# Last stage of a decoder step: LayerNorm rows broadcast by DMA instead of spread by TensorE, and part of VectorE's row work moved to GpSimd

## The chip, the cores and the metric

One NeuronCore of a Trainium2 chip runs the whole kernel. The metric is device time in microseconds of one execution; a profiled execution also leaves a trace of every instruction. Engines: PE (TensorE), DVE (VectorE), ACT (ScalarE), POOL (GpSimd), SP (SyncE, which here only issues DMAs and waits).

## The reference, cut to what matters

The kernel is one layer of a hybrid decoder for 512 prompt tokens and 32 sample tokens, all in float32. The stage that changes computes what follows the first LayerNorm:

```python
x = layer_norm(DN_ALPHA * x + mix, ln_g[0], ln_b[0])
x = layer_norm(DN_ALPHA * x + hier_moe(x, ...), ln_g[1], ln_b[1])      # 32 experts, top 2 of one group
ple = jax.nn.sigmoid(x @ w_pg) * (p_i @ w_pp)
x = layer_norm(DN_ALPHA * x + ple, ln_g[2], ln_b[2])
```

`x` is 544 x 1024, `w_pg` 1024 x 1024. The products with `w_pg` are made from high and low halves of both sides (three matmuls for one), so each side is first split into a rounded copy and the rest.

## The kernel before, in words

The prompt's tokens are handled as NT = 4 tiles of 128 rows x 1024 columns (`x1s[0]` to `x1s[3]`), the 32 sample tokens as one tile of 128 x 256 (`x1q`, with the helpers that end in `_q`).

**The expert phase** (`expert_phase`) is one critical section: each engine runs its own hand-written program, ordered by semaphores, and the planner sees the section as one block. Weights lie in four slots; SyncE refills them, and once a slot's last expert is done (`late`), it loads what the next stage needs into the freed room: the four `x1s` tiles, LN1's gain `gain1`, and one half of `w_pg`. TensorE does gate and up products (L302), a transpose (L307) and the down product (`psY`, L316) of each expert; GpSimd scatters each result to `ybuf` in DRAM. Behind the last expert TensorE spreads LN2's gain and shift over 128 partitions (`spread_half`, L148: a matmul with a broadcast column of the identity, from the 48 x 128 tile `gb`), four halves into PSUM, and ScalarE copies each out (L449). VectorE multiplies the four `x1s` tiles by `gain1` (L526). Each engine raises `fin` when it is done; SyncE waits for the last scatters (L237), for its late loads, and for `fin` of all four (L240). Only then does any engine go on.

**The last stage** follows in the planner's own order (`issue_after` places some instructions behind others of the same engine). SyncE loads the experts' results for each tile (`rows_of_experts`, two tiles of 128 x 1024 for each t), the other half of `w_pg`, and the embeddings' products. The order of the work:

- TensorE runs products that nothing reads (`keep_busy`, L2115: eight matmuls of 256 columns, which the trace lists as 16 records), spreads LN3's gain and shift (`spread`, L2107 for ScalarE's copies), and runs eight more.
- ScalarE casts the first half of `w_pg` in eight chunks of 128 x 512 (L577) and VectorE takes the rest (L578): the split of chunk k.
- `moe_norm(0)`: VectorE adds the two experts' results (L2130, L2131; the second leaves the row sum `total`), ScalarE makes the sum of squares (L2122), GpSimd the power -1/2 (L2124), VectorE the two last operations (L1771, L1772).
- `turn(0)`: TensorE transposes the tile (L2145), ScalarE and VectorE split it (L2146, L2147).
- The second half of `w_pg` is split (L2245, L2247), then `moe_norm(1)`.
- For each tile `embed_norm`: 2 x 8 x 3 matmuls (`three`, L690 to L692), a sigmoid, the product with the embedding, LN3 and the store; between them the norm and the turn of the next tiles and the sample rows.

Of the kernel before, what the change touches and what calls it, by code (L numbers as in the profile page):

```python
# [9 lines left out]
F32 = mybir.dt.float32  # L10
# [9 lines left out]
P = 128  # L20
# [122 lines left out]

def spread_half(pe, ident, rows, out, first):

    n = rows.shape[0]
    for k in range(4):
        m = pe.matmul(out[:, P * k:P * (k + 1)], ident[0:n, first + k:first + k + 1].to_broadcast([n, P]), rows[:], start=True, stop=True)  # L148
    return m


def expert_phase(tc, pool, psum, ident, meta, slots, x1, W, w, ybuf, spare, gcol, late, rows, spreads, xs, any_):

# [25 lines left out]
    names = [f"{n}{i}" for n in ("gu", "gv", "wd", "we") for i in range(NB)]  # L179
    names += "gh gi gx tx c4 cx gu xa xb rb se sc ra sl hh th ch dn cy iy y0 y1 y2 y3 al fin gz".split()  # L180
    with tc.tile_critical(no_gpsimd_drain=True):
# [188 lines left out]
        pe.matmul(psY[:], ident, any_, start=True, stop=True)  # L370
        npp, full, gap = value(pe, 80, NB, 32), value(pe, 81, 0, 32 // NB - 1), value(pe, 84, 0, NB - 1)
        with pe.If(full > 0):
            with pe.Fori(0, full) as a:
                for s in range(NB):
                    items_of(a, s, pe.snap(a * NB + s), turn_before(a) if s == 0 else
                             lambda i: down_of(s - 1, i, pe.snap(a + 1)))
        full1 = pe.snap(full + 1)
        for s in range(NB):
# [15 lines left out]
            else:  # L394
                items_of(full, s, p, prev)
        it = value(pe, 82, 1, 66)
        pe.wait_ge(S["hh"], pe.snap(it + 1))
        transpose_h()
        down_of(NB - 1, it, full1)

        halves = [(out[:, 512 * i:512 * (i + 1)], which + 4 * i) for out, which in spreads for i in range(2)]
        banks = [psX[:, 4 * i:4 * i + 4].rearrange("p k t -> p (k t)") for i in range(2)]
        for n, (_, which) in enumerate(halves):
            if n > 1:
                pe.wait_ge(S["sc"], n - 1)
            spread_half(pe, ident, rows, banks[n % 2], which).then_inc(S["se"], 1)
        pe.sem_inc(S["fin"], 1)
# [38 lines left out]
        act.activation(out=tiny, in_=gcol[:, 0, 0:1], func=AF.Sigmoid)  # L446
        for n, (out, _) in enumerate(halves):
            act.wait_ge(S["se"], n + 1)
            act.copy(out=out, in_=banks[n % 2]).then_inc(S["sc"], 1)  # L449
        act.wait_ge(S["sc"], len(halves))  # L450
        act.sem_inc(S["fin"], 1)
# [81 lines left out]
def tile_decoder_step(ctx: ExitStack, tc: tile.TileContext, *aps):  # L533
# [1113 lines left out]
    gcol8 = const.tile([P, 2, KD], F32, name="gcol8")  # L1647
    gb = const.tile([6 * KD, P], F32, name="gb")
    const.tile([P, 8], F32, name="edgel")
# [61 lines left out]
    act.mul(out=shift1, in_=shift1, mul=0.5)  # L1711
    for j, n in enumerate(("ln_g", "ln_b")):
        gp.dma_start(out=gb[24 * j:24 * j + 24], in_=A[n][0].rearrange("i (k d) -> (i k) d", k=KD))

# [118 lines left out]
    with ExitStack() as scope:  # L1833
# [203 lines left out]
        with tc.issue_after(table.ins):  # L2037
# [17 lines left out]
    gbq = [t.rearrange("p (j d) -> p j d", j=2) for t in gbq]  # L2055
    gain2, shift2, gain3, shift3 = (r_p[:, i] for i in range(4))

    pg_half = lambda i: (pg_in[i], A["w_pg"][0, :, 512 * i:512 * (i + 1)].rearrange("(k p) f -> p k f", p=P))
    late = [(0, [(x1s[t], x1d[t * P:(t + 1) * P], "rb") for t in range(NT)] + [(gain1, A["ln_g"][0, 0].partition_broadcast(P), "rb"),
                                                                                         (*pg_half(0), "al")])]  # L2060
    spreads = [(gain2, 8), (shift2, 32)]
    with ExitStack() as scope:

        SP_ = pool("spare", stack=scope)
        spare = SP_.tile([P, D], F32, name="xg"), SP_.tile([P, 2, KD, P], F32, name="xg4")
        gp.indirect_dma_start(out=spare[0], out_offset=None, in_=x1d[:], in_offset=bass.IndirectOffsetOnAxis(ap=tok0[:, 0:1], axis=0))
        expert_phase(tc, pool("xwork", side="right", stack=scope), pool("expp", space=PSUM, stack=scope), ident, meta,
                     (tok, yrow, ywt, shift1, gain1), x1d[:], w_tiles, w_e, ybuf[:], spare, gcol8, late, gb, spreads, x1s,
                     keep[:, 0:256])
# [30 lines left out]

    def spread(out, i):

        for half in range(2):
            cs = slice(512 * half, 512 * (half + 1))
            po = ps2.tile([P, 512], F32, name="po")
            m = spread_half(pe, ident, gb, po, i + 4 * half)
            act.copy(out=out[:, cs], in_=po)  # L2107
        return m

    def keep_busy(n, behind=None):  # L2110

        idle = ps2.tile([P, 256], F32, name="pp", bufs=1)
        with tc.issue_after(behind.ins) if behind else nullcontext():
            for _ in range(n):
                m = pe.matmul(idle, ident, keep[:, 0:256], start=True, stop=True)  # L2115
        return m

# [8 lines left out]
    def moe_norm(t):  # L2126
        x2 = x1s[t]
        y1, y2 = held[t]
        total = TL.tile([P, 1], F32, name="total", bufs=4)
        dve.tensor_tensor(out=x2, in0=x2, in1=y1, op=ALU.add)  # L2130
        dve.scalar_tensor_tensor(out=x2, in0=y2, scalar=1.0, in1=x2, op0=ALU.mult, op1=ALU.add, accum_out=total)  # L2131
        stats = full_stats(x2, total, y2, EPS2)
        if t:
# [61 lines left out]
    def moe_norm_q():  # L2195
        dve.tensor_tensor(out=x1q, in0=x1q, in1=gbq[0][:, 0], op=ALU.mult)
        for i in range(2):
            dve.tensor_tensor(out=x1q, in0=x1q, in1=yq[:, i], op=ALU.add)
        norm_q(x1q, 0)
# [19 lines left out]
    sy.dma_start(out=pg_half(1)[0], in_=pg_half(1)[1])  # L2219
    rows_of_experts(1)  # L2220
    for out, src in ((embeds[:, 0:512], pld[P:2 * P, 512:]), (embeds[:, 512:512 + D], pld[2 * P:3 * P])):
        sy.dma_start(out=out, in_=src)
    rows_of_experts(2)
    rows_of_experts(3)
    for out, src in ((embeds[:, 512 + D:], pld[3 * P:4 * P]), (pls, plsd[:]), (x1q, x1d[SEQ:].rearrange("t (q d) -> q t d", q=4)),
                     *((yq[:, i], ybuf[NG * i + SEQ:NG * (i + 1)].rearrange("t (q d) -> q t d", q=4)) for i in range(2))):
        dma = sy.dma_start(out=out, in_=src)
    busy = keep_busy(8)
    for k in range(KD):
        cast = split_from(pg(k, 0, 0, 512), pg(k, 1, 0, 512), pg_in[0][:, k])  # L2230
    with tc.issue_after(busy.ins), tc.issue_after(cast.ins):
        spread(gain3, 16)
        busy = spread(shift3, 40)
    keep_busy(8, busy)
    with tc.issue_after(dma.ins):
# [6 lines left out]
    for k in range(KD):  # L2242
        H, L, src = pg(k, 0, 512, D), pg(k, 1, 512, D), pg_in[1][:, k]
        with tc.issue_after(high.ins):
            act.copy(out=H, in_=src)  # L2245
        with tc.issue_after(low.ins):
            lows = dve.tensor_tensor(out=L, in0=src, in1=H.bitcast(F32), op=ALU.subtract)  # L2247
    for t in range(1, NT + 2):
        if t <= NT:
            if t < NT:  # L2250
                with tc.issue_after(applied.ins if t > 1 else lows.ins):
                    behind, applied = moe_norm(t)
            if t == NT - 2:
                with tc.issue_after(applied.ins):
                    moe_norm_q()
# [39 lines left out]
```

## Time and profile before

| | us |
|---|---|
| median of 3 runs | 1138.86 (1135.3 to 1141.66) |
| the profiled execution: time | 1140.12 |
| its span, from first to last instruction | 1138.2 |
| PE busy | 1046.4 (92%) |
| DVE busy | 487.4 (43%) |
| ACT busy | 346.7 (30%) |
| POOL busy | 249.9 (22%) |

Times of the profile count from the start of the span. The shares are means over stages that differ: the expert phase waits for weights, the last stage (from about 1040 us) for one engine after another. A row of the timeline gives start, duration, engine, line, operation and operands, and in brackets the idle time before it with what ended it. The granted clock is the share of its full clock that TensorE was given.

### The profile page before, as it was taken

How to read it: one execution, taken by the hardware profiler on the slowest of the kernel's cores; microseconds unless marked ns; L12 is line 12 of the kernel's file. 1: busy time of each engine (PE TensorE's matmuls, PEld its weight loads, DVE VectorE, ACT ScalarE, POOL GpSimd, SP SyncE). 2: the span in 40 equal slices, each digit the busy share in tenths (PEclk: the TensorE clock that was granted, in tenths of full speed). 3: DMA queues.
4: the chain of work that ended last, by engine and by line, in shares of the span. 5: the costliest groups of instructions: out<-in, count | busy, mean ns of one | idle time of the engine just before them, and what ended most of it. 6: DMA issues, size and time to landing. Idle time of an engine off the chain costs nothing.

```text
span 1138.2 us, 26943 instructions
## 1 busy us (share of the span) xinstructions
PE 1046.4 (92%) x10391; PEld 817.4 (72%) x10392; DVE 487.4 (43%) x1255; ACT 346.7 (30%) x702; POOL 249.9 (22%) x379
## 2 busy tenths in 40 slices
PE   9999999999999999999999877696998979977987
PEld 8988999999877779999989444343555545544765
DVE  5545543456545556554665511110111111112787
ACT  5411123232666665323213111110222111111531
POOL 5000001301346562223301102210222212211021
PEclk9999999999999999999999889987999999988888
DMA  7222222224214334654396989999999999997711
GB/s 249 76 75 75 75 74 75 79 75 132 80 37 149 111 114 142 208 158 102 122 413 256 372 310 414 422 416 425 415 422 418 420 420 419 422 419 304 282 46 61
DMA packets 99296, 264.18 MB, mean 232 GB/s; under 512 B 11470, under 2 KB 58852, under 8 KB 85364
## 3 DMA queue, kind: packets, MB, share of 16 engines
q1 hardware_dynamic: 84868, 234.05, 53.9%
q0 software_dynamic: 9696, 25.31, 6.2%
q10 hardware_dynamic: 4656, 3.77, 1.1%
q8 instruction: 53, 0.87, 0.3%
q14 instruction: 23, 0.19, 0.1%
HBM read 248.96 MB, written 20.13 MB: 236 GB/s over the span
## 4 chain that ended last, share of the span: by engine, by line
PE 75%; DMA 10%; SPq 7%; issue 3%; DVE 3%; ACT 1%; DVEq 0%; POOL 0%; ACTq 0%; POOLq 0%
PE pj L690 14%; PE pj L692 13%; PE pj L691 13%; PE psG L302 10%; SPq L135 5%; PE psY L316 5%; DMA gu3b<-in_w_eu_dram 5%; PE tp L1285 2%; DMA w<-in_w_eu_dram 2%; DMA w2b<-in_w_eu_dram 2%; SPq L141 2%; PE sp L1331 1%; PE nm L1319 1%; PE sp L748 1%; PE po L692 1%
## 5 line engine op out<-in xcount | busy, mean ns | idle before, releaser
L690 PE MATMUL pj<-xH,wH 128*128 128x256 f32 (+1 forms) x672 | 197.6, 294 | 0.1
L692 PE MATMUL pj<-xH,wL 128*128 128x256 f32 (+1 forms) x672 | 197.4, 294 | 0.0
L691 PE MATMUL pj<-xL,wH 128*128 128x256 f32 (+1 forms) x672 | 195.6, 291 | 0.0
L577 ACT CAST wH<-raw 128x1024 fp32r<-128x1024 f32 x76 | 79.7, 1049 | 232.3 <-PE pj L691 148.1
L690 PEld LDWEIGHTS pj<-xH,wH 128*128 128x128 f32 x672 | 126.5, 188 | 5.5 <-issue 3.8
L692 PEld LDWEIGHTS pj<-xH,wL 128*128 128x128 f32 x672 | 126.4, 188 | 5.5 <-issue 5.1
L691 PEld LDWEIGHTS pj<-xL,wH 128*128 128x128 f32 x672 | 127.0, 189 | 2.0 <-issue 1.5
L578 DVE TENSOR_TENSOR wL<-raw,wH 128x1024 fp32r<-128x1024 f32 x76 | 95.2, 1252 | 69.4 <-ACT wH L577 69.2
L302 PE MATMUL psG<-w,xT 128*32 128x256 f32 x1152 | 77.1, 410 | 25.1 <-issue 16.8
L434 ACT ACTIVATE sg<-psG 128x128 f32<-128x128 f32 x50 | 13.9, 277 | 270.3 <-PE psG L302 270.3
L465 DVE COPY hT<-psH 128x128 f32<-128x128 f32 x50 | 14.6, 292 | 153.3 <-PE psH L307 151.4
L302 PEld LDWEIGHTS psG<-w,xT 128*32 128x32 f32 x1152 | 38.4, 116 | 55.2 <-issue 36.1
L1307 POOL TENSOR_SCALAR lg<-lg,sm 128x256 f32<-128x256 f32 (+1 forms) x64 | 55.8, 886 | 32.6 <-DVE sm L1304 28.6
L460 DVE COPY xT<-xg 128x256 f32 x49 | 14.5, 295 | 111.8 <-PE psG L302 111.8
L265 POOL DMA_INDIRECT ybuf<-ysb,idy x50 | 49.6, 992 | 45.8 <-POOL idy L262 40.1
L302 PE MATMUL psG<-gu3a,xT 128*32 128x256 f32 x576 | 36.7, 395 | 15.5 <-DMA gu3a<-in_w_eu_dram 9.5
L472 DVE SCALAR_TENSOR_TENSOR ysb<-psY,ywt,r_p 128x256 f32<-128x256 f32 x50 | 24.2, 483 | 56.8 <-PE psY L316 56.8
L690 PE MATMUL pj<-wH,xH 128*128 128x256 f32 x160 | 47.3, 296 | 0.0
L416 ACT ACTIVATE xg<-psX,gcol 128x128 f32 (+1 forms) x100 | 36.4, 469 | 33.6 <-PE psX L295 33.6
L692 PE MATMUL pj<-wH,xL 128*128 128x256 f32 x160 | 44.8, 280 | 0.0
L691 PE MATMUL pj<-wL,xH 128*128 128x256 f32 x160 | 44.7, 280 | 0.0
L302 PE MATMUL psG<-gu3b,xT 128*32 128x256 f32 x576 | 38.2, 410 | 6.1 <-DMA gu3b<-in_w_eu_dram 6.1
(615 smaller groups left out, 2265.3 us busy)
## 6 DMA issues: line engine op xcount, KB each, us to landing
w<-in_w_eg_dram SPq DMA_DIRECT2D x26, 1024.0 KB, 20.6
w<-in_w_eu_dram SPq DMA_DIRECT2D x26, 1024.0 KB, 23.1
w<-in_w_ed_dram SPq DMA_DIRECT2D x26, 1024.0 KB, 24.6
raw<-in_w_in_dram SPq DMA_DIRECT2D x22, 1024.0 KB
w2d<-in_w_ed_dram SPq DMA_DIRECT2D x14, 1024.0 KB, 24.4
r_p<-in_w_ed_dram SPq DMA_DIRECT2D x14, 1024.0 KB, 22.4
w2a<-in_w_eg_dram SPq DMA_DIRECT2D x7, 1024.0 KB, 22.4
w2a<-in_w_eu_dram SPq DMA_DIRECT2D x7, 1024.0 KB, 26.6
```

The costliest lines, as they stand in the source:

```text
L135: return [eng.dma_start(out=W[s][half][:, i], in_=w[i][bass.ds(e, 1)].rearrange("a (p k) f -> (a p) k f", p=P)[:, ks]) for i in range(2)]
L265: gp.indirect_dma_start(out=ybuf.rearrange("t (q d) -> (t q) d", q=4), out_offset=bass.IndirectOffsetOnAxis(ap=idy[:, r:r + 1], axis=0), i ...
L302: m = pe.matmul(psG[32 * q:32 * q + 32], xT[:, k], W[s][half][:, :, kh, P * q:P * q + P], start=k == 0, stop=k == KD - 1)
L316: m = pe.matmul(psY[32 * q:32 * q + 32], hT[:, 32 * k:32 * k + 32], W[s][2][:, k, 256 * q:256 * q + 256], start=k == 0, stop=k == 3)
L416: m = act.activation(out=out, in_=psX[:, k], func=AF.Identity, bias=gcol[:, 1, k:k + 1], scale=gcol[:, 0, k:k + 1])
L472: dve.scalar_tensor_tensor(out=ysb[:, r], in0=psY[:], scalar=ywt[:, bass.ds(i1, 1)], in1=shift, op0=ALU.mult, op1=ALU.add).then_inc(S["cy" ...
L577: act.copy(out=H, in_=src)
L578: return eng.tensor_tensor(out=L, in0=src, in1=H.bitcast(F32), op=ALU.subtract)
L690: pe.matmul(out, lh(k), rh(k), start=start and i == 0, stop=False)
L691: pe.matmul(out, lh(k), rl(k), start=False, stop=False)
L692: pe.matmul(out, ll(k), rh(k), start=False, stop=stop and i == len(ks) - 1)
L1307: gp.tensor_scalar(out=lg[:, par, j, 0:nk], in0=lg[:, par, j, 0:nk], scalar1=sm[:, 2, par, j:j + 1], scalar2=None, op0=ALU.mult)
```

## The change

In the expert phase the spreads go, with their copies and semaphores. LN2's gain and shift come by DMA, each as one row read 128 times, queued by SyncE behind the last experts of slots 1 and 2; SyncE waits for them (`al`) at the end. TensorE issues ten products that nothing reads, and loads one register earlier. VectorE multiplies only `x1s[0]` by `gain1` there.

In the last stage LN3's gain and shift come by DMA, behind the second tile's results. The first batch of products grows from 8 to 14; the second batch is made from `total` of the first tile and so waits for it. GpSimd takes over: `gain1` on the other three tiles, the splits of chunks 5 to 7 of the first half and 4 to 7 of the second, the first add of tiles 2 and 3, and three operations on the sample rows. `moe_norm(1)` is placed behind VectorE's fourth split of the second half instead of the eighth.

```diff
@@ expert_phase
+        it = value(pe, 82, 1, 66)
         with pe.If(full > 0):
...
-        it = value(pe, 82, 1, 66)
         pe.wait_ge(S["hh"], pe.snap(it + 1))
         transpose_h()
         down_of(NB - 1, it, full1)
-        for n, (_, which) in enumerate(halves):
-            if n > 1:
-                pe.wait_ge(S["sc"], n - 1)
-            spread_half(pe, ident, rows, banks[n % 2], which).then_inc(S["se"], 1)
+        for _ in range(10):
+            pe.matmul(psX[:, 0:2].rearrange("p k t -> p (k t)"), ident, any_, start=True, stop=True)
         pe.sem_inc(S["fin"], 1)
...
-        for n, (out, _) in enumerate(halves):
-            act.wait_ge(S["se"], n + 1)
-            act.copy(out=out, in_=banks[n % 2]).then_inc(S["sc"], 1)
-        act.wait_ge(S["sc"], len(halves))
         act.sem_inc(S["fin"], 1)
@@ tile_decoder_step
-    gb = const.tile([6 * KD, P], F32, name="gb")
...
-    for j, n in enumerate(("ln_g", "ln_b")):
-        gp.dma_start(out=gb[24 * j:24 * j + 24], in_=A[n][0].rearrange("i (k d) -> (i k) d", k=KD))
...
-    gain2, shift2, gain3, shift3 = (r_p[:, i] for i in range(4))
+    gain2, shift2, gain3, shift3 = row(W1, 11), row(w2a, 2), r_p[:, 2], r_p[:, 3]
...
-                                                                                         (*pg_half(0), "al")])]
-    spreads = [(gain2, 8), (shift2, 32)]
+                                                                                         (*pg_half(0), "al")]),
+            (1, [(gain2, A["ln_g"][0, 1].partition_broadcast(P), "al")]), (2, [(shift2, A["ln_b"][0, 1].partition_broadcast(P), "al")])]
...
-                     (tok, yrow, ywt, shift1, gain1), x1d[:], w_tiles, w_e, ybuf[:], spare, gcol8, late, gb, spreads, x1s,
+                     (tok, yrow, ywt, shift1, gain1), x1d[:], w_tiles, w_e, ybuf[:], spare, gcol8, late, x1s[0:1],
...
-    def keep_busy(n, behind=None):
+    def keep_busy(n, by=ident):
         idle = ps2.tile([P, 256], F32, name="pp", bufs=1)
-        with tc.issue_after(behind.ins) if behind else nullcontext():
-            for _ in range(n):
-                m = pe.matmul(idle, ident, keep[:, 0:256], start=True, stop=True)
-        return m
+        for _ in range(n):
+            pe.matmul(idle, by, keep[:, 0:256], start=True, stop=True)
@@ moe_norm
-        dve.tensor_tensor(out=x2, in0=x2, in1=y1, op=ALU.add)
+        if t < 2:
+            dve.tensor_tensor(out=x2, in0=x2, in1=y1, op=ALU.add)
         dve.scalar_tensor_tensor(out=x2, in0=y2, scalar=1.0, in1=x2, op0=ALU.mult, op1=ALU.add, accum_out=total)
+        if t == 0:
+            keep_busy(8, total[:, 0:1].to_broadcast([P, P]))
@@ moe_norm_q
-        dve.tensor_tensor(out=x1q, in0=x1q, in1=gbq[0][:, 0], op=ALU.mult)
+        gp.tensor_tensor(out=x1q, in0=x1q, in1=gbq[0][:, 0], op=ALU.mult)
         for i in range(2):
-            dve.tensor_tensor(out=x1q, in0=x1q, in1=yq[:, i], op=ALU.add)
+            gp.tensor_tensor(out=x1q, in0=x1q, in1=yq[:, i], op=ALU.add)
@@ the last stage
     rows_of_experts(1)
+    for out, m in ((gain3, A["ln_g"]), (shift3, A["ln_b"])):
+        sy.dma_start(out=out, in_=m[0, 2].partition_broadcast(P))
...
-    busy = keep_busy(8)
+    keep_busy(14)
+    gp.tensor_tensor(out=x1s[1], in0=x1s[1], in1=gain1, op=ALU.mult)
     for k in range(KD):
-        cast = split_from(pg(k, 0, 0, 512), pg(k, 1, 0, 512), pg_in[0][:, k])
-    with tc.issue_after(busy.ins), tc.issue_after(cast.ins):
-        spread(gain3, 16)
-        busy = spread(shift3, 40)
-    keep_busy(8, busy)
+        low = split_from(pg(k, 0, 0, 512), pg(k, 1, 0, 512), pg_in[0][:, k], gp if k > 4 else dve)
+        if k == 4:
+            cast = low
...
         with tc.issue_after(low.ins):
-            lows = dve.tensor_tensor(out=L, in0=src, in1=H.bitcast(F32), op=ALU.subtract)
+            lows = (dve if k < 4 else gp).tensor_tensor(out=L, in0=src, in1=H.bitcast(F32), op=ALU.subtract)
+        if k == KD // 2 - 1:
+            halfway = lows
     for t in range(1, NT + 2):
         if t <= NT:
             if t < NT:
-                with tc.issue_after(applied.ins if t > 1 else lows.ins):
+                with tc.issue_after(applied.ins if t > 1 else halfway.ins):
                     behind, applied = moe_norm(t)
+            if t == 1:
+                for later in (2, 3):
+                    with tc.issue_after(behind.ins):
+                        gp.tensor_tensor(out=x1s[later], in0=x1s[later], in1=gain1, op=ALU.mult)
+                        gp.tensor_tensor(out=x1s[later], in0=x1s[later], in1=yall[2 * later], op=ALU.add)
```

More of the change, by code (lines that the diff above doesn't have):

```diff
@@ L141, in load_dn, with expert_phase @@
     return eng.dma_start(out=W[s][2][:, ks], in_=w[2][bass.ds(e, 1)].rearrange("a (k p) d -> p (a k) d", p=P)[:, ks])
[L144 to L148, printed above, removed]
-    return m
-def expert_phase(tc, pool, psum, ident, meta, slots, x1, W, w, ybuf, spare, gcol, late, rows, spreads, xs, any_):
+def expert_phase(tc, pool, psum, ident, meta, slots, x1, W, w, ybuf, spare, gcol, late, xs, any_):
     nc = tc.nc
@@ L179, in expert_phase @@
     names = [f"{n}{i}" for n in ("gu", "gv", "wd", "we") for i in range(NB)]
-    names += "gh gi gx tx c4 cx gu xa xb rb se sc ra sl hh th ch dn cy iy y0 y1 y2 y3 al fin gz".split()
+    names += "gh gi gx tx c4 cx gu xa xb rb ra sl hh th ch dn cy iy y0 y1 y2 y3 al fin gz".split()
     with tc.tile_critical(no_gpsimd_drain=True):
@@ L399, in expert_phase @@
         down_of(NB - 1, it, full1)
-        halves = [(out[:, 512 * i:512 * (i + 1)], which + 4 * i) for out, which in spreads for i in range(2)]
-        banks = [psX[:, 4 * i:4 * i + 4].rearrange("p k t -> p (k t)") for i in range(2)]
-        for n, (_, which) in enumerate(halves):
-            if n > 1:
-                pe.wait_ge(S["sc"], n - 1)
-            spread_half(pe, ident, rows, banks[n % 2], which).then_inc(S["se"], 1)
+        for _ in range(10):
+            pe.matmul(psX[:, 0:2].rearrange("p k t -> p (k t)"), ident, any_, start=True, stop=True)
         pe.sem_inc(S["fin"], 1)
@@ L2099, in embedding @@
         return kept[:, n, lo % 512:lo % 512 + hi - lo] if n < 3 else embeds[:, 512 * (n - 3) + lo % 512:512 * (n - 3) + lo % 512 + hi - lo]
[L2101 to L2108, printed above, removed]
-    def keep_busy(n, behind=None):
+    def keep_busy(n, by=ident):
         idle = ps2.tile([P, 256], F32, name="pp", bufs=1)
-        with tc.issue_after(behind.ins) if behind else nullcontext():
-            for _ in range(n):
-                m = pe.matmul(idle, ident, keep[:, 0:256], start=True, stop=True)
-        return m
+        for _ in range(n):
+            pe.matmul(idle, by, keep[:, 0:256], start=True, stop=True)
     def full_stats(x, total, junk, eps):
```

## The prediction

> **What bounds the kernel now.** I read the page first, then the chain of waits from 1040 us on, then what SyncE's DMA queue waited for, then the timelines of VectorE and GpSimd, and last the grouped rows of GpSimd and the granted clock by stretches. The change touches only what comes after the last expert, so the sum is made on that stretch. The page's own measure, then the chain there (start, duration, what):
>
> ```profile
> span 1138.2 us, 26943 instructions
> ```
>
> ```profile
> 1040.45 3.45 issue
> 1044.80 3.64 PE psY L316 x32
> 1048.44 7.14 PE psX L148 x32
> 1055.60 0.59 ACT r_p L449
> 1056.26 0.02 SPq L240
> 1056.85 5.58 PE pp L2115 x16
> 1062.44 3.81 PE po L148 x32
> 1066.24 3.65 PE pp L2115 x16
> 1069.89 0.45 PE tp L2145 x4
> ```
>
> The last expert's second product (psY) ends at 1048.4; the spreads of LN2's rows (psX) and ScalarE's last copy of them then hold the section until 1056.2, SyncE passes its last wait at 1056.26, and all engines go on at 1056.85. I call this moment the opening. After it TensorE does nothing that counts until the first rows are normalised and turned (tp). The columns of the next rows are start, duration, engine, line, operation, and in brackets the idle time before it and what ended it:
>
> ```profile
> 1057.92 4.90 DVE L578 TENSOR_TENSOR pg<-w,pg 128x512 fp32r<-128x512 f32 x8 [4.01 <-ACT pg L577]
> 1062.75 1.22 DVE L2130 TENSOR_TENSOR w<-w,w 128x1024 f32<-128x1024 f32 x1
> 1065.27 0.15 DVE L2121 TENSOR_SCALAR fmv<-total 128x1 f32<-128x1 f32 x1
> 1068.16 1.41 DVE L1772 SCALAR_TENSOR_TENSOR w<-w,fmv,r_p 128x512 f32<-128x512 f32 x2
> 1072.19 4.90 DVE L2247 TENSOR_TENSOR pg<-w,pg 128x512 fp32r<-128x512 f32 x8
> 1077.01 1.22 DVE L2130 TENSOR_TENSOR w<-w,w 128x1024 f32<-128x1024 f32 x1
> 1083.82 1.28 DVE L1772 SCALAR_TENSOR_TENSOR w<-w,fmv,r_p 128x1024 f32<-128x1024 f32 x1
> 1085.24 1.09 PE L2145 MATMUL tp<-keep,w 128*128 128x128 f32 x4 [2.79 <-DVE w L1772]
> 1103.17 0.50 PE L692 MATMUL po<-pg,xT 128*128 128x512 f32 x1 [0.59 <-DVE xT L2147]
> ```
>
> VectorE sets both starts: eight splits (0.61 each), then the norm of the first rows, and after the turn eight more splits and the norm of the second rows, for which TensorE stands idle 2.79 us. From 1085 on TensorE has work in hand, with one wait of 0.59 for VectorE. So what counts is when the stage opens, and when the second rows are ready. The idle time also costs clock, as the granted clock by stretches shows (stretch, its length, PE busy, clock, DMA share, GB/s):
>
> ```profile
> 1043.90:1060.90 17.00, 15.28 (x75) 0.51 0.31 107
> 1060.90:1084.80 23.90, 21.31 (x112) 0.99 0.82 310
> 1084.80:1091.40 6.60, 6.16 (x18) 0.50 0.23 73
> ```
>
> **The opening.** The spreads go: 7.14 us of TensorE and the copy behind it. The ten products that take their place raise no semaphore, and nothing waits for their end before the opening. VectorE keeps one of the four multiplies L526, so it is done 3 x 1.16 = 3.5 us sooner. What is late next is a transfer.
>
> ```profile
> 1049.28 4.64 DVE L526 TENSOR_TENSOR w<-w,r_s 128x1024 f32<-128x1024 f32 x4 [0.20 <-issue]
> 1029.18 1.95 SPq L230 DMA_DIRECT2D r_s<-in_ln_g_dram  x1
> 1031.18 1.19 SPq L230 DMA_DIRECT2D w<-in_w_pg_dram  x1
> r_s<-in_ln_g_dram SPq DMA_DIRECT2D x1, 512.0 KB, 16.3
> w<-in_w_pg_dram SPq DMA_DIRECT2D x1, 2048.0 KB, 20.0
> SPq L240 <- ACTq L451: 3.2, 1, 3.2
> ```
>
> SyncE waited 3.2 us for ScalarE, so all its other waits, the last scatter among them, were over by 1056.3 - 3.2 = 1053.1. The half of w_pg landed at 1031.18 + 20.0 = 1051.2; LN1's gain, issued just ahead, at 1029.18 + 16.3 = 1045.5. So 2 MB took 5.7 us behind it, 1.4 us per 512 KB. The change puts two such rows behind w_pg, gain2 once slot 1's last product is done and shift2 once slot 2's is (1040.5), and SyncE now waits for them: 1051.2 + 2 x 1.4 = 1054.0 instead of 1056.3. The queue has nothing else of the section behind these two, so only the exit waits. I take **-2.4** for the opening (bounds: -3.2, where the scatter is last; 0, where shift2 takes gain1's 16.3 us from 1040.6 and lands at 1056.9). The register load that TensorE now does ahead of the loop shortens the 3.45 us of "issue" by something, which moves the scatter, not the rows: nothing.
>
> **GpSimd's price.** No two-operand row of 128x512 or 128x1024 runs on GpSimd in this trace. The nearest:
>
> ```profile
> L950 POOL TENSOR_TENSOR sigA<-sigA,sigB 128x288 f32<-128x288 f32 x8 | 6.5, 807 | 17.5 <-DVE sigB L949 17.5
> L950 POOL TENSOR_TENSOR sigA<-sigA,sigB 128x256 f32<-128x256 f32 x8 | 5.9, 736 | 10.7 <-DVE sigB L949 10.7
> ```
>
> 71 ns more for 32 elements is 2.2 ns an element; the estimate is 1.3 us for 512 and 2.44 us for 1024, twice VectorE's 0.61 and 1.14. Beside VectorE that would be harmless if both ran freely. They don't:
>
> ```profile
> L578 DVE TENSOR_TENSOR pg<-w,pg 128x512 fp32r<-128x512 f32 x8 | 4.9, 685 | 4.0 <-ACT pg L577 4.0
> 645.29 0.83 DVE L2003 TENSOR_TENSOR At<-minus,lo 128x640 f16<-128x640 f32 x1
> 645.29 1.89 DVE L2003 TENSOR_TENSOR At<-minus,lo 128x640 f16<-128x640 f32 x2
> 645.32 1.18 POOL L2000 TENSOR_TENSOR Bt<-Be,keep 128x200 f16<-128x200 f32 x1 [4.74 <-DVE lo L2001]
> 510.85 1.23 DVE L578 TENSOR_TENSOR wL<-raw,wH 128x1024 fp32r<-128x1024 f32 x1 [0.55 <-ACT wH L577]
> 516.97 1.45 DVE L578 TENSOR_TENSOR wL<-raw,wH 128x1024 fp32r<-128x1024 f32 x1 [0.53 <-ACT wH L577]
> 516.52 0.81 POOL L950 TENSOR_TENSOR sigA<-sigA,sigB 128x288 f32<-128x288 f32 x1 [2.60 <-DVE sigB L949]
> ```
>
> GpSimd's 128x200 (0.62 by the slope) took 1.18: it stood until VectorE's first L2003 ended at 646.12. Then VectorE's second stood: rows in a row overlap a little (eight splits of 0.685 in 4.90, 0.08 each), so a pair of 0.83 would be 1.58; it took 1.89, 0.31 us for 200 elements, 1.6 ns each. The same split L578 takes 1.23 alone and 1.45 where it starts inside GpSimd's L950. So the two take turns on operands in SBUF, instruction by instruction, and each GpSimd row holds VectorE for 0.8 us (512) or 1.6 (1024) where VectorE has such work in hand. I take 1.6 ns an element because L2003 is the one row with VectorE queued behind a waiting GpSimd; the bounds are nothing (GpSimd fits into VectorE's pauses) and the whole of 1.3 and 2.44.
>
> The Trainium skill, page "SBUF — State Buffer", section "Who interferes with whom", has a rule against this change: a VectorE instruction with two SBUF inputs and a GpSimd instruction that reads SBUF exclude each other, and the second to start blocks until the first has finished. The trace agrees on the exclusion (1.45 against 1.23); by the whole instruction the sum would be the slower rival's below.
>
> **First rows.** At the opening GpSimd starts gain1 on x1s[1], about 0.3 us in, and the port is free at about 2.0; VectorE's first split was ready at 1.07 (1057.92 - 1056.85), so +1.0. Three of eight splits leave VectorE: -1.8. They come back as holds when ScalarE has cast chunks 5 to 7, just while VectorE does its last splits and the add L2130: 3 x 0.8 = +2.4. The total comes at 8.4 + 1.6 = 10.0 us after the opening, the norm +1.6. In the kernel before, the norm's first half ended at 1068.9 and the turn began some 0.8 later, behind products that end at 1069.9; the new eight products start with the total and last 3.65, as long as the norm needs from there, and behind their wait for the total only the turn is queued. So the first turn comes **+0.8** against the opening. The second batch of products (14 for 8) ends 6.4 to 9.8 us after the opening (28 records at 3.65/16 or 5.58/16), in front of that total: nothing, if the gate stays open.
>
> **Second rows.** Four splits leave VectorE: **-2.4**. GpSimd's four start once ScalarE has cast chunk 4; one falls into VectorE's pause for the sum of squares, three hold it: **+2.4**. Their own end matters to nobody: TensorE reads chunk 7's low half last. Queued behind them on GpSimd is the power L2124 of the second norm, and behind that power the multiply and add of rows 2 and 3, four of 2.44 us.
>
> ```profile
> 614.31 0.55 POOL L583 TENSOR_TENSOR lmv<-lmv,npow 128x1 f32<-128x1 f32 x1 [0.85 <-DVE lmv L582]
> 1082.19 1.51 POOL L2124 TENSOR_TENSOR fmv<-fmv,npow 128x1 f32<-128x1 f32 x1 [14.18 <-DVE fmv L2123]
> ```
>
> The power ended at 1083.70 (1.51 instead of 0.55, another such turn), VectorE's L1772 began 0.12 later. GpSimd's next row follows without a semaphore between and should have the port first: **+1.6** on the very instruction that TensorE waits for (0 if VectorE is first).
>
> **Later.** Rows 2 must pass GpSimd (4.9 us) and VectorE, then a power behind rows 3; TensorE then has 11 us of the second rows' products, which cover it. VectorE's L2131 of rows 2 now waits for GpSimd's add; the low halves of the second turn may be queued behind that wait, up to 2 us, taken as nothing because those products start well after it. VectorE is rid of two adds and the sample rows' three, so its 0.59 us wait at 1103 should go: **-0.6**. gain3 and shift3 add 1 MB to SyncE's queue ahead of the embeddings and rows 2 and 3; the first to want them comes 20 us later: nothing, or 2 x 1.4 = 2.8 if that cover is gone. GpSimd's two small loads of the spreads' source, long before the experts, go: nothing. TensorE's idle time before the second rows grows by about 1.5, and the gate shuts as before.
>
> Sum: -2.4 + 0.8 - 2.4 + 2.4 + 1.6 - 0.6 = **-0.6 us**. The profiled execution took 1140.12 (span 1138.2 and 1.9 around it); the median of the runs is 1138.86, so the forecast is **1138.2**. What a measurement of this kernel can tell from no change is about 0.5%, 5.7 us.
>
> **Rivals.** *Faster: VectorE is hardly held*, because GpSimd's rows find its pauses. Then the first turn comes 1.8 + 0.8 earlier, the second rows 2.4 more, with the opening and the 0.6: -8.0. TensorE's idle time shrinks to some 0.4 us and the 6.6 us at half clock go, 3.3 more: -11.3, **1127.5**. For it: VectorE does have pauses of 1.3 us for each sum of squares; against it: the rows above. Chance 0.30.
>
> *The opening stays*, because shift2 lands as late as the spreads ended: 1138.2 + 2.4 = **1140.6**. For it: gain1 took 16.3 us; against it: nothing is queued behind it that late. Chance 0.13.
>
> *Slower: the port is held for whole instructions.* The place is the start of the stage: first split at 2.75 instead of 1.07 (+1.7), -1.8, 3 x 1.3: +3.8, so the total comes 12.2 us after the opening, 2.4 to 5.8 after the 14 products' end. From an idle stretch of about 3.4 us (1040.45, after which the clock is 0.51) the gate shuts: eight products at 5.58 instead of 3.65 stand before the turn. First turn 3.0 + 2.0, second rows -2.4 + 3.9 + 2.4, opening -2.4: +6.5, and 0.9 for transposes at half clock: **1146**. It decides from a hold of about 2 us a row of 1024 on. For it the row with 1.45; against it the 0.31 of L2003. Chance 0.17.
>
> **Numbers.** Forecast 0.40 and the opening rival 0.13 lie within 5.7 us: same 0.53, faster 0.30, slower 0.17. The range reaches from the faster rival to nearly the slower one, 1128 to 1145; the likeliest case alone, by its bounds (0 to -3.2 at the opening, 0 for VectorE first), has 1136 to 1141.
>
> **What would show it.** In the profile after: the opening near 1054.5; GpSimd rows of 2.4 and 1.3 us; VectorE splits and L2130 longer than 0.7 and 1.22 where they meet them; the second norm's last instruction about 1.6 longer; TensorE idle 3 to 5 us before the second turn. The prediction is wrong where those VectorE durations are unchanged, or where a wait for shift2 or for GpSimd's power ends the chain instead.

## The result, and the profile after

| | before | after |
|---|---|---|
| median of the runs, us | 1137.92 (6 runs, 1135.28 to 1141.66) | 1149.29 (6 runs, 1147.65 to 1152.18) |
| profiled execution: time, span | 1140.12, 1138.2 | 1152.18, 1150.4 |

The ratio is 1.0101, 95% interval 1.0081 to 1.0121. The changed kernel is about 11 us slower; the forecast was 1138.2, the range 1128 to 1145. The profiled execution is the longest of the six after.

The chain of waits of the changed kernel (start, duration, what), in the stretch that was shown of before:

```profile
1045.82 3.12 issue
...
1058.61 0.44 PEldq L173
1059.34 0.63 ACT pg L561
...
1070.60 6.35 PE pp L2086 x16
1076.95 0.45 PE tp L2118 x4
...
1090.59 3.37 DVE w L1753
1094.09 1.10 PE tp L2118 x4
```

The products of the last stage open at 1059.24. Set beside the rows of before, the 12.2 us between the spans come from five stretches:

| stretch | before | after | difference |
|---|---|---|---|
| start to the end of the next-to-last down product | 1040.45 | 1045.82 | +5.4 |
| from there to the opening | 16.40 | 13.42 | -3.0 |
| opening to the first turn | 13.04 | 17.71 | +4.7 |
| first to second turn | 15.35 | 17.14 | +1.8 |
| second turn to the end of the span | 52.96 | 56.31 | +3.3 |

VectorE's timeline of the changed kernel shows what grew (start, duration, engine, line, operation):

```profile
1059.99 8.06 DVE L562 TENSOR_TENSOR pg<-w,pg 128x512 fp32r<-128x512 f32 x5 [4.43 <-ACT pg L561]
1081.65 2.32 DVE L2101 TENSOR_TENSOR w<-w,w 128x1024 f32<-128x1024 f32 x1
1084.01 2.20 DVE L2102 SCALAR_TENSOR_TENSOR w<-w,w 128x1024 f32<-128x1024 f32 x1
1090.59 3.36 DVE L1753 SCALAR_TENSOR_TENSOR w<-w,fmv,w2a 128x1024 f32<-128x1024 f32 x1 [0.45 <-POOL fmv L2094]
1096.44 2.60 DVE L2138 SCALAR_TENSOR_TENSOR w<-w,w 128x512 f32<-128x512 f32 x1
1099.64 3.42 DVE L2102 SCALAR_TENSOR_TENSOR w<-w,w 128x1024 f32<-128x1024 f32 x1
```

The same operations took 0.61 a split, 1.22 (L2130, now L2101) and 1.28 (L1772, now L1753) before. The other two were these rows of the kernel before (L2165, now L2138, and L2131, now L2102):

```profile
1086.15 0.68 DVE L2165 SCALAR_TENSOR_TENSOR w<-w,w 128x512 f32<-128x512 f32 x1
1086.76 1.22 DVE L2131 SCALAR_TENSOR_TENSOR w<-w,w 128x1024 f32<-128x1024 f32 x1
```

None of the added time is a wait for a semaphore: it lies inside the instructions. GpSimd's timeline of the same kernel has a row beside each of them:

```profile
1059.51 2.36 POOL L2204 TENSOR_TENSOR w<-w,r_s 128x1024 f32<-128x1024 f32 x1
1062.64 4.86 POOL L562 TENSOR_TENSOR pg<-w,pg 128x512 fp32r<-128x512 f32 x3 [0.77 <-ACT pg L561]
1081.19 7.87 POOL L2221 TENSOR_TENSOR pg<-w,pg 128x512 fp32r<-128x512 f32 x4 [7.96 <-ACT pg L2219]
1090.53 5.63 POOL L2232 TENSOR_TENSOR w<-w,r_s 128x1024 f32<-128x1024 f32 x2
1096.12 2.37 POOL L2233 TENSOR_TENSOR w<-w,w 128x1024 f32<-128x1024 f32 x1
```

L1753 was ready at 1090.59, 0.06 us behind the start of GpSimd's multiply of tile 2, and stood for nearly the whole of it. What all of this costs is read from the busy time of the last stage, from the opening to the end of the span (start and end, length, then busy time of PE, PEld, DVE, ACT and POOL with the count of instructions, granted clock, DMA share, GB/s); first the kernel before, then the changed one:

```profile
1056.80:1138.20 81.40, 69.29 (x382) 56.17 (x382) 64.11 (x130) 28.68 (x52) 11.46 (x11) 0.90 0.37 136
```

```profile
1059.20:1150.40 91.20, 70.78 (x362) 56.27 (x362) 71.62 (x118) 26.86 (x48) 40.18 (x26) 0.87 0.35 133
```

Twelve instructions left VectorE, and it is busy 7.5 us more. Seven splits of 0.61, two adds of 1.22 and three operations on the sample rows (0.42 each in experiment 10) make 8.0 us that are gone, so some 15 us of the 71.6 are standing still, over GpSimd's 15 added rows: about 1 us each.

### The profile page after: what moved, and what is told of

Its sections match the earlier page's. It is cut to its first block, busy times and chain, and to the rows that moved or that the text cites. A ratio compares the mean times of both kernels' runs of the same rounds, so it can differ in the third digit from the quotient of the medians.

```text
span 1150.4 us, 26885 instructions
## 1 busy us (share of the span) xinstructions
PE 1047.1 (91%) x10359; PEld 814.7 (71%) x10360; DVE 491.5 (43%) x1240; ACT 342.5 (30%) x694; POOL 277.6 (24%) x392
## 4 chain that ended last, share of the span: by engine, by line
PE 72%; SPq 9%; DMA 8%; issue 4%; DVE 4%; ACT 1%; POOL 1%; PEld 1%; DVEq 0%; ACTq 0%; PEldq 0%
PE pj L674 13%; PE pj L676 13%; PE pj L675 13%; PE psG L294 10%; SPq L135 5%; DMA gu3b<-in_w_eu_dram 4%; PE psY L308 4%; SPq L141 3%; PE tp L1269 2%; DMA w2b<-in_w_eu_dram 2%; PE sp L1315 1%; PE nm L1303 1%; PE sp L732 1%; PE pj L1833 1%; DMA wg_in<-in_w_in_dram 1%
## 5 line engine op out<-in xcount | busy, mean ns | idle before, releaser
L294 PE MATMUL psG<-gu3a,xT 128*32 128x256 f32 x576 | 37.7, 404 | 15.5 <-DMA gu3a<-in_w_eu_dram 9.4
```

What stands on the lines that cost most here:

```text
L294: m = pe.matmul(psG[32 * q:32 * q + 32], xT[:, k], W[s][half][:, :, kh, P * q:P * q + P], start=k == 0, stop=k == KD - 1)
```

## The experiments

Theories: **port** (each GpSimd row stops VectorE's two-operand rows for nearly its length, and VectorE sets the stage), **clock** (the eight products behind the total and the shut gate, that is TensorE's granted clock at about half, cost the time), and for the 5.4 us ahead of the stage **loads** (taking out two small loads changes the order that the planner gives the start) or accident. What was measured, all against runs of the kernel before on the same chip (stretches from each profile, by TensorE's timeline):

| kernel | median, us | ratio, 95% interval | experts begin | opening to 1st turn | 1st to 2nd turn | 2nd turn to end |
|---|---|---|---|---|---|---|
| before | 1137.92 | 1 | 660.8 | 12.9 | 15.5 | 53.0 |
| after | 1149.29 | 1.0101 (1.0081, 1.0121) | 663.0 | 17.6 | 17.3 | 56.3 |
| 1 rows on VectorE | 1139.38 | 1.0013 (0.9995, 1.0032) | 660.5 | 13.4 | 15.5 | 52.2 |
| 2 before, GpSimd rows | 1152.42 | 1.0115 (1.0090, 1.0140) | 657.9 | 22.3 | 17.3 | 54.4 |
| 3 loads kept | 1147.76 | 1.0073 (1.0048, 1.0098) | 657.8 | 16.8 | 17.3 | 54.7 |
| 4 no products behind total | 1146.43 | 1.0069 (1.0044, 1.0094) | 663.0 | 14.9 | 18.1 | 54.7 |
| 5 before, load moved | 1137.59 | 1.0009 (0.9998, 1.0021) | 658.2 | 13.0 | 15.5 | 51.8 |
| 6 = 1, load back | 1138.31 | 1.0006 (0.9993, 1.0018) | 660.7 | 13.4 | 15.5 | 52.2 |
| 7 rows 2, 3 later | 1148.20 | 1.0088 (1.0071, 1.0105) | 661.9 | 16.4 | 15.2 | 59.5 |
| 8 = 1, filled | 1138.33 | 1.0007 (0.9994, 1.0021) | 663.1 | 12.5 | 15.5 | 52.2 |
| 9 first turn's rows alone | 1143.75 | 1.0050 (1.0032, 1.0068) | 660.8 | 17.6 | 15.5 | 53.7 |
| 10 rows 2, 3 alone | 1145.03 | 1.0064 (1.0043, 1.0084) | 660.0 | 13.4 | 17.5 | 55.7 |
| 11 = 1, unread rows | 1146.06 | 1.0074 (1.0054, 1.0094) | 661.9 | 17.2 | 17.1 | 52.7 |
| 12 second splits alone | 1138.90 | 1.0011 (0.9995, 1.0027) | 663.7 | 11.8 | 15.4 | 52.7 |
| 13 = 1, loads kept | 1134.98 | 0.9974 (0.9960, 0.9988) | 660.0 | 11.8 | 15.6 | 51.2 |
| 14 = 8, loads kept | 1139.47 | 1.0018 (1.0003, 1.0033) | 658.9 | 11.8 | 18.8 | 52.4 |
| 15 before, loads late | 1140.59 | 1.0025 (1.0012, 1.0038) | 663.5 | 12.9 | 15.5 | 53.2 |

The clock alone moves the column of the first turn. Up to that turn experiments 1 and 12 hold the same work, and their eight products behind the total took 5.38 and 3.69 us, each after 1.92 us of idle time, at a granted clock of 0.76 and 1.00 around them. That is the 1.6 us between 13.4 and 11.8, so a difference of this size in this column says nothing about an edit.

**1. All rows back on VectorE.**

```diff
-    gp.tensor_tensor(out=x1s[1], in0=x1s[1], in1=gain1, op=ALU.mult)
-        low = split_from(pg(k, 0, 0, 512), pg(k, 1, 0, 512), pg_in[0][:, k], gp if k > 4 else dve)
+        low = split_from(pg(k, 0, 0, 512), pg(k, 1, 0, 512), pg_in[0][:, k], dve)
-            lows = (dve if k < 4 else gp).tensor_tensor(...)
+            lows = dve.tensor_tensor(...)
```

and so for tiles 2 and 3, the sample rows and the gain in the expert phase.

> The changed kernel with every row that went to GpSimd given back to VectorE; the broadcast rows by DMA, the ten, the 14 and the eight products stay. Port theory (each GpSimd row stops VectorE for nearly its whole length): VectorE's splits are 0.61 us again, the total comes about 8.4 us after the opening instead of 11.2, the first turn about 13 to 14 instead of 17.7, the second rows 28 to 29.5 instead of 34.8, and the 3.3 us lost after them go as well: 1138 to 1141. Clock theory (the eight products behind the total and the shut gate cost the time, the rows are nearly free): VectorE gains four splits of work in front of the second rows and the kernel stays at 1147 to 1151. In both the part ahead of the stage stays where the changed kernel has it (next-to-last down product's end near 1045.8), if its loss comes from the loads that were taken out far ahead.

1139.38: the port theory's value. About 10 of the 11.4 us are the rows on GpSimd. VectorE's busy time in the stage is that of before again, 64.1 us:

```profile
1054.70:1135.80 81.10, 66.74 (x362) 53.11 (x362) 64.12 (x130) 26.55 (x48) 10.75 (x11) 0.94 0.40 150
```

**2. The kernel before with the GpSimd rows alone** (the same lines, the other way).

> The kernel before with the GpSimd rows alone: spreads, copies, loads and the products of before all stay. Port theory: the second rows come some 4 to 6 us later after the opening than in the kernel before (28.4), and 2 to 3 more are lost behind them: 1143 to 1147. Clock theory: no products wait for the total here, so nothing is lost: 1136 to 1140. Ahead of the stage the order of all instructions is that of the kernel before, so the next-to-last down product should end near 1040.5; if it ends as late as 1044 to 1046, that loss varies by itself and does not come from the loads that were taken out.

1152.42, worse than both theories had it. The first turn comes 22.3 us after the opening: here TensorE's second spread and eight products stand before it, and the spread waits for a copy that ScalarE does only behind the late sum of squares, as TensorE's timeline of this kernel shows:

```profile
1069.46 3.78 PE L148 MATMUL po<-gb,keep 48*128 48x128 f32 x16 [5.75 <-ACT r_p L2107]
1073.17 5.54 PE L2115 MATMUL pp<-keep 128*128 128x256 f32 x16
```

So no products that wait for a total are needed for the loss.

**3. The two small loads kept** in the changed kernel (`gb` and its two `gp.dma_start`, read by nothing).

> The changed kernel with the 48 x 128 tile and its two small GpSimd loads left in, read by nothing. This puts every instruction ahead of the expert phase back into the order of the kernel before. If taking the loads out is what delayed the part ahead of the stage: next-to-last down product's end 1040.5 to 1041.5 instead of 1045.8 and the time 1143 to 1145. If that delay is of another origin (the register load moved ahead of the loop, or the weights' stream by itself): 1147 to 1151.

Inconclusive: the median is 1.5 us lower than after and still in the range of the other origin, the intervals overlap, and its runs spread over 6 us (1141.55 to 1147.98). Experiments 13 to 15 take the question up again.

**4. No products behind the total.**

```diff
-        if t == 0:
-            keep_busy(8, total[:, 0:1].to_broadcast([P, P]))
```

> The changed kernel without the eight products that wait for the total. Clock theory (they stand in the turn's way at half clock): the first turn starts 0.8 us after the norm's first half, about 15.5 us after the opening instead of 17.7: 1147 or a little less. Rival (the gate is shut anyway, so that what is not done in these products is paid in the turn and in the first product rows): 1148 to 1152, no gain. By the port theory VectorE's rows stay as long as in the changed kernel.

1146.43; the first turn comes 2.6 us sooner, the second stretch is 0.8 longer. So in the changed kernel these products do stand in the way, by some 2 to 3 us. The late total leaves TensorE 5.05 us idle ahead of them, and the eight then take 6.35 us at a granted clock of 0.58, instead of 3.65 in the kernel before.

**5 and 6. The register load.** In 5 `it = value(pe, 82, 1, 66)` alone is moved ahead of the loop in the kernel before; in 6 it goes back behind the loop in the first experiment's kernel.

> The kernel before with one edit: TensorE reads its register (the count of experts) ahead of the loop. The profiles of the four runs so far show the last stage itself, from the last down product on, 7.2 us longer in the changed kernel and 2.0 us shorter with the rows back on VectorE, but their medians lie some 3.5 to 4 us higher than that against the kernel before. If the moved load slows the expert phase: 1141 to 1142. If it does not, and the place of that loss is elsewhere or an accident of the profiled runs: 1137 to 1139.

> The changed kernel with the rows back on VectorE (as in the first run) and the register load back behind the loop: the same question from the other side. If the moved load costs 3.5 us: 1135.5 to 1136.5 instead of 1139.4. If not: 1138.5 to 1140.

1137.59 and 1138.31: the load moves nothing that can be measured.

**7. Tiles 2 and 3 behind the second norm.**

```diff
+                with tc.issue_after(behind.ins):
+                    seen = gp.tensor_copy(out=mark, in_=x1s[1][:, 0:1])
                 for later in (2, 3):
-                    with tc.issue_after(behind.ins):
+                    with tc.issue_after(seen.ins):
```

> The changed kernel with one edit: GpSimd's multiply and add of tiles 2 and 3 wait for the end of the second tile's norm (a copy of one column stands ahead of them), where before they ran right behind its power and met VectorE's last norm instruction. Port theory, with a hold of a whole instruction: that instruction takes 1.28 us again instead of 3.36 and the second turn comes 2.1 us sooner after the first (15.2 instead of 17.3); at the end 1 to 2.1 us remain, because the rows of tile 2 come later: 1147 to 1148.5. Rival (VectorE is held by something else, or GpSimd's next row takes the port anyway): 17.3 stays, 1149 to 1150.

1148.20. The instruction is 1.28 again and the second turn 2.1 us sooner; then the hold is met elsewhere, and the rest is 3.2 us longer. VectorE's timeline of this kernel:

```profile
1086.44 1.28 DVE L1753 SCALAR_TENSOR_TENSOR w<-w,fmv,w2a 128x1024 f32<-128x1024 f32 x1 [0.45 <-POOL fmv L2094]
1096.23 3.40 DVE L2102 SCALAR_TENSOR_TENSOR w<-w,w 128x1024 f32<-128x1024 f32 x1 [3.06 <-POOL w L2236]
```

**8. The first experiment's kernel, filled**: `keep_busy(20)` for 14, and six products that wait for the second tile's total.

> The rows back on VectorE, the first batch of products 20 instead of 14, and six products that wait for the second tile's total ahead of the second turn, where TensorE stood idle 2.79 us. Clock theory: no idle stretch is left before the first total (1.9 us) and before the second turn, so the eight products take 3.65 us instead of 5.38 (the first turn 1.3 us sooner) and the transposes and products after the second turn run at full clock (up to 3.3 us of the 6.6 us at half clock): 1135 to 1136.5 against 1139.4. Rival (the time at half clock is covered, VectorE decides what comes later): 1138 to 1140.

1138.33, the rival's value. The gate does stay open behind the second turn, and the stretch from there to the end is 52.2 us with it as without. Busy times behind the second turn, first of experiment 1, then of this one:

```profile
1083.60:1092.00 8.40, 8.34 (x32) 6.22 (x33) 7.16 (x16) 3.55 (x6) 2.24 (x2) 0.80 0.22 73
```

```profile
1086.80:1095.00 8.20, 7.04 (x33) 5.50 (x34) 6.95 (x16) 3.45 (x6) 2.24 (x2) 1.00 0.26 85
1095.00:1111.00 16.00, 15.28 (x72) 12.26 (x71) 14.33 (x29) 4.54 (x8) 2.38 (x2) 1.00 0.08 33
```

A granted clock of 1.00 instead of 0.80 only gives TensorE more idle time, because VectorE is busy 14.3 of the next 16 us. Experiment 1's 0.80 over 8.4 us is 1.7 us short of the full clock, so about half of the 3.3 us that the prediction's faster rival credited to the clock was at stake here, and none of it came; the other half is not tested.

**9, 10 and 12. One group of GpSimd rows at a time**, the others on VectorE: the gain of tile 1 and the splits 5 to 7 (9), the multiply and add of tiles 2 and 3 (10), the second half's splits 4 to 7 (12).

> Broadcast rows by DMA and, of the GpSimd rows, only those ahead of the first turn: the gain on the second tile and the splits of chunks 5 to 7 of the first half. All else on VectorE. Port theory: the first turn 17 to 17.5 us after the opening as in the changed kernel (13.4 with all rows on VectorE), the second 15.5 behind it; since VectorE sets what follows as well, the 4 us go through to the end: 1142 to 1143.5. Rival (work behind covers it): 1138 to 1140.

> Broadcast rows by DMA and, of the GpSimd rows, only the multiply and the add of tiles 2 and 3, right behind the power of the second norm. Port theory: the second norm's last instruction takes 3.3 us instead of 1.28, the second turn comes 17.5 us after the first instead of 15.5, and VectorE is held again behind it (in the changed kernel the stretch from there to the end is 4 us longer than with all rows on VectorE), though it is rid of two multiplies and two adds: 1141 to 1144. Rival (the rows are cheap once nothing else is moved): 1138 to 1140.

> Broadcast rows by DMA and, of the GpSimd rows, only the splits of chunks 4 to 7 of the second half. Port theory: four splits (2.4 us) leave VectorE, and the add, the sum and the norm that stand beside them are held by 1.0 to 1.1 us each: the second turn 15.5 to 16.5 us after the first, 1139 to 1141. If the four were free: 13 us after the first, 1136 to 1137.

Against experiment 1 they cost 4.4, 5.6 and -0.5 us, together 9.5; all groups at once, with the three sample rows that stand in none of them, cost 9.9. 9 and 10 lie 0.3 and 1.0 us above the port theory's ranges, 12 lies 0.1 below its range. In 10 the second norm's last instruction stands again, and so does the row behind it:

```profile
1082.06 3.28 DVE L1753 SCALAR_TENSOR_TENSOR w<-w,fmv,w2a 128x1024 f32<-128x1024 f32 x1
1085.26 2.83 DVE L2138 SCALAR_TENSOR_TENSOR w<-w,w 128x512 f32<-128x512 f32 x1
```

In 12 four splits leave (2.4 us), and three instructions beside them grow by about 1 us each: nothing is won.

**11. Rows that nobody reads**, added to experiment 1: three `gp.tensor_tensor` of 128x512 beside the first half's splits, four `gp.tensor_copy` of 128x512 beside the second half's.

> All rows on VectorE, and GpSimd given rows whose results nobody reads: three two-operand rows of 128x512 beside the splits of the first half, and four copies (one operand) of 128x512 beside those of the second half. So VectorE's and TensorE's own work is that of the first run, and any delay is the meeting on the port. Port theory: the eight splits of the first half take 4.9 + 3 x 1.1 = 8.2 us, the first turn comes 3.3 later. For the copies two readings: any GpSimd row that reads SBUF stops VectorE's two-operand rows for its length (the second half's splits 4.9 + 4 x 0.6 or more), or only two-operand rows do (4.9 stays). Time 1142 to 1145. If GpSimd's rows are no cause by themselves: splits 4.9 and 4.9, 1138 to 1140.

1146.06, 1.1 us above the port theory's range. This is the cleanest measure, since nothing was taken from VectorE. Its splits, first in experiment 1, then in this kernel:

```profile
1055.45 4.91 DVE L562 TENSOR_TENSOR pg<-w,pg 128x512 fp32r<-128x512 f32 x8 [1.89 <-ACT pg L561]
1070.59 4.89 DVE L2219 TENSOR_TENSOR pg<-w,pg 128x512 fp32r<-128x512 f32 x8
```

```profile
1057.30 8.15 DVE L562 TENSOR_TENSOR pg<-w,pg 128x512 fp32r<-128x512 f32 x8 [2.67 <-ACT pg L561]
1076.21 6.53 DVE L2222 TENSOR_TENSOR pg<-w,pg 128x512 fp32r<-128x512 f32 x8
```

Three two-operand rows cost (8.15 - 4.91)/3 = 1.08 us each. Four copies cost (6.53 - 4.89)/4 = 0.41 each: a row with one operand holds VectorE too, for less.

**13, 14 and 15. The loads, again.** 13 and 14 are experiments 1 and 8 with the two loads kept; 15 is the kernel before with the two loads taken from GpSimd's queue and given to SyncE's. In the program they stand just ahead of the expert phase; the planner issued them at 10.67 and 11.11 us, where GpSimd had issued them at 13.12 and 13.63. In its profile ScalarE and GpSimd run the first 100 us in the order that they have in the changed kernel.

> The first run's kernel (broadcast rows by DMA, all rows on VectorE) with the tile of the spreads and its two small GpSimd loads left in, read by nothing, so that all instructions ahead of the expert phase stand in the order of the kernel before. Loads theory (taking the two loads out makes the planner order the start of the kernel otherwise, and the expert phase begins some 3 us later: 660.0 to 663.7 us in the ten profiles without them, 657.8 to 660.8 in the four with them): 1136 to 1137, the 2 us that the last stage is shorter now show. Accident theory (the start varies by itself, the kernels share one distribution): 1138.5 to 1140 as without the loads.

> The same with the 20 products and the six ahead of the second turn. Loads theory: 1135 to 1136.5, below both kernels. Accident theory: 1138 to 1139.

> The kernel before with its two small loads moved from GpSimd's queue near the start to SyncE's queue just ahead of the expert phase: the start of the kernel then has the order that it has in the changed kernel, and the last stage is that of the kernel before. Loads theory: the expert phase begins at 660 to 663.7, 1140 to 1141.5. Accident theory: 1137 to 1138.5.

15 bears out the loads theory, about 3 us more than before (by the interval 1.4 to 4.3). 13 is 4.4 us below experiment 1, more than that theory gave, and it does not isolate the start of the kernel. The profiled executions of 1 and 13 are 3.0 us apart: 0.5 lies ahead of the opening, 1.6 in front of the first turn, where the eight products took 3.69 us instead of 5.38, and 1.0 behind the second turn, where the planner gave VectorE another order (the third turn comes 11.3 us behind the second instead of 13.4). 14 came out at the accident theory's value, but it fell out of the plan: the planner put the eight products between the two halves of the first turn, so the second turn came 3 us later, and it tells nothing about the loads:

```profile
1065.07 0.66 PE L2120 MATMUL tp<-keep,w 128*128 128x128 f32 x4 [1.20 <-DVE w L1756]
1065.56 3.62 PE L2089 MATMUL pp<-keep,total 128*128 128x256 f32 x16
1069.02 0.60 PE L2120 MATMUL tp<-keep,w 128*128 128x128 f32 x4
```

Part of the mechanism is in TensorE's longest wait in the first 60 us (line, releaser, total, times, longest). In the changed kernel, then in 15, then in 13:

```profile
PE pj L674 <- ACT qkT L829: 1.6, 1, 1.6
```

```profile
PE pj L690 <- ACT qkT L845: 1.5, 1, 1.5
```

```profile
PE pj L598 <- DVE mp L1042: 1.0, 1, 1.0
```

Without the two loads on GpSimd's queue the planner puts ScalarE's cast of `mrs` and a table load in another place ahead of a row `qkT` that TensorE wants: the row starts at 33.78 us in the changed kernel and at 32.37 before, and TensorE waits 1.5 to 1.6 us that it doesn't wait in the kernel before or in 13. This wait is in all eleven profiles without the two loads on that queue and in none of the six with them, and it lasts: the first store of an `x1d` tile is issued at 601.6 to 602.6 us in the eleven and at 600.2 to 600.7 in the six, 1.7 us apart on average. So this much of the loss ahead of the stage is shown. How the rest of the 3 us arises was not traced.

Experiment 13, broadcast rows by DMA and none of the added rows on GpSimd, is the fastest kernel here: 0.26% below the kernel before.

## Why the prediction was wrong

- **"The change touches only what comes after the last expert, so the sum is made on that stretch"** failed. "GpSimd's two small loads ... go: nothing" cost 1.7 us that every profile shows at 600 us, and about 3 us in all by experiment 15; the profiled run shows 5.4 us. The rest may be spread between runs: without the two loads on GpSimd's queue the experts begin anywhere from 660.0 to 663.7 and the next-to-last down product ends anywhere from 1040.0 to 1047.4; with them, from 657.8 to 660.8 and from 1036.2 to 1040.8.
- **The opening, -2.4**: right in size, -3.0 in the profile, and alone -1.9 in experiment 13 (14.53 us from the next-to-last down product's end instead of 16.40; the other kernels without the spreads have 12.7 to 15.0). The reason was another: SyncE's last waits were not for the rows but, in 13, for the last scatter, and, in the changed kernel, for TensorE, whose ten products, at a granted clock of 0.81, ran to 1059.0. "Nothing waits for their end" was wrong by 0.4 us, as SyncE's waits show:

```profile
SPq L173 <- PEq L173: 0.4, 1, 0.4
```

- **The hold, 0.8 us for 512 and 1.6 for 1024**, is the term that was mis-sized. Measured: 1.08 for 512 (11), and 3.36 - 1.28 = 2.08 for 1024. The one row with VectorE queued, L2003, gave 1.6 ns an element; it is 2.0 to 2.1. The rule of the Trainium skill quoted in the prediction, page "SBUF — State Buffer", section "Who interferes with whom", that the second waits until the first has finished, fits better: 2.08 of the 2.36 that such a multiply takes (L2204).
- **First turn, +0.8**: measured +4.7. The total came 11.2 us after the opening (1070.45) instead of 10.0; the slower rival had 12.2. "Nothing, if the gate stays open" failed next: it shut, and the eight products cost some 2 to 3 us (4). So the price was 1.2 us of hold beyond the estimate, and the products that this lateness put in the way. The slower rival's condition, an idle stretch of some 3.4 us, does not decide it: behind 1.92 us the eight products took 5.38 in experiment 1 and 3.69 in 12. (The 14 products, which the prediction calls the second batch, are the first.)
- **Second rows, +1.6**: measured +1.8, and the place was right: GpSimd's next row took the port ahead of VectorE's last norm instruction. The hold there was 2.1, and alone it makes the stretch 17.5 instead of 15.5 (10). The pair -2.4 + 2.4 came out at -0.1 (12), in part by luck: the three held rows grew by 3.0, and the planner put two rows of the first tile's embedding step into the pause for the sum of squares.
- **Later, -0.6**: measured +3.3. "L2131 of rows 2 now waits for GpSimd's add ... up to 2 us, taken as nothing" failed: that instruction (now L2102) stood for 3.42 us and, ahead of it, L2138 for 2.60, because GpSimd works on tiles 2 and 3 just when VectorE has the first tile's embedding step and the third tile's norm in hand. One of the second turn's low halves was queued behind L2138 and came at 1098.97. TensorE did not cover it; VectorE sets this stretch too (8).
- **The slower rival** had the mechanism and 1146; it lacked the later stretch and the loads.

## What to carry to other kernels

Work moved from VectorE to GpSimd is not taken away when both read SBUF: here each GpSimd row of 512 or 1024 columns cost VectorE 1.1 or 2.1 us where VectorE had such rows in hand, as much as VectorE needs for 1.7 to 1.8 of them itself, so by these numbers it can only pay where VectorE is idle. Removing an operation that is "hidden" far ahead can move others when a planner orders the program: compare the order of the whole program, not only the stage that was edited. And before crediting a faster clock, see which engine ends the stretch: TensorE at full clock gained nothing behind VectorE.

## What the runs showed of the hardware

GpSimd's rows need not have two operands: its copy of 128x512, 0.92 us long between VectorE's rows (four in 3.66), cost VectorE 0.41 us, a two-operand row of that size 1.08. And VectorE's rows that read one side from PSUM were not held. In experiment 10 VectorE's two splits of a turned tile (L2120, one operand in PSUM) ran beside GpSimd's add, and the next row, both operands in SBUF, stood; VectorE first, then GpSimd:

```profile
1090.24 1.27 DVE L2120 TENSOR_TENSOR xT<-tp,xT 128x512 fp32r<-128x512 f32 x2
1091.44 2.27 DVE L2102 SCALAR_TENSOR_TENSOR w<-w,w 128x1024 f32<-128x1024 f32 x1
```

```profile
1090.27 2.36 POOL L2232 TENSOR_TENSOR w<-w,w2a 128x1024 f32<-128x1024 f32 x1
```

Both splits took 1.27 us together, as in experiment 1 without GpSimd (1.29); L2102 took 2.27 instead of 1.22 and went on when GpSimd's add ended at 1092.63.
